# A decoder trunk on one core: decays' subtractions behind C B^T on VectorE, next weights behind the last operands, attention's output in natural column order

## The chip, the cores and the metric

The kernel runs on one core of a Trainium2 chip. Its engines are TensorE (PE, matrix products; PEld is its weight load), VectorE (DVE), ScalarE (ACT), GpSimd (POOL) and SyncE (SP, which issues the DMAs here). The metric is the device time of one execution in microseconds; the time of a kernel is the median of its runs. The profile is of one execution of its own.

## The reference

The input is one sequence of 512 tokens of width 1024, in float32. Two residual layers follow one another, each with a mixer and a gated convolutional feed-forward (FFN), each part behind an RMS norm; a last RMS norm ends it.

```python
for i in range(DEPTH):                       # DEPTH = 2
    h = rmsnorm(x, mix_norm_w[i])
    if i % 2 == 0: x = x + dilated_attention_mixer(...)   # 8 heads, 3 groups, dilations 1, 4, 16
    else:          x = x + ssd_mixer(...)                 # Mamba-2: 32 heads in 8 groups, chunks of 128
    h = rmsnorm(x, ffn_norm_w[i])
    x = x + conv_ffn(h, ...)                 # (silu(gate) * up) @ w_down, behind a causal convolution of 3
return rmsnorm(x, final_norm_w)
```

What matters of the Mamba-2 mixer: for each group the projections x, z, B and C; a causal convolution of four taps and SiLU on x, B and C; and then, for every chunk and head,

```python
seg    = a_cs[:, :, :, None] - a_cs[:, :, None, :]     # differences of running sums
lmat   = exp(where(causal, seg, -inf))
cb     = einsum("bcign,bcjgn->bcijg", cm, bm)          # C B^T of the group
y_diag = einsum("bcijgr,bcjgrp->bcigrp", cb[..., None] * lmat, xdt)
```

with the carried states added, the result gated by silu(z), normed per group and multiplied by w_out.

## The kernel before

**Products in three parts.** Every weight matrix comes as a unit of 128 x 1024 float32. `load_unit` (line 116) issues its DMA on SP into a buffer `raw` (4 of them), makes the high part `hi` by a cast on ACT (line 125) and the low part `lo = raw - hi` on DVE, or on the engine that `low` names (line 126; 5 buffers each). An operand is split likewise into `xh` (ACT, line 203) and `xl` (DVE, line 204). A product is then three matmuls (`mm3`, line 136): hi x xh, hi x xl, lo x xh. A tile of 128 x 512 over the width of 1024 is 8 x 3 = 24 matmuls, accumulated in one of three banks of PSUM called `mm`; there are three more called `aux` and two called `side`.

**Order.** The order on PE is written out by hand (`manual_schedule`). On the other engines a scheduler orders the instructions: of those that are ready by its own timing, the one first in the program. Each engine then works through its queue in that order. `tc.issue_after(ins)` puts what is traced inside it, as far as it is on the engine of `ins`, behind `ins` in that engine's queue; it sets an order and no wait, and binds no other engine, SP included. `queued(name)` (line 715) does this for the last instruction kept under a name.

**Attention.** Tokens are held in another order than the natural one: a column of the 512 stands for (n, r, l) = (block, residue, place). `attend(h)` (line 392) makes one head's scores, softmax and values; at its end line 491 copies the bank `pg` of the dilated groups to `o`, line 492 adds the bank `po`, and lines 494 and 495 split `o`. After the heads, the output projection `wo` adds to the residual `xr`, whose columns are natural: line 579 does it with a stride of 4 elements on `xr`, and `prep` splits `xr[m]` for the FFN.

**Entries.** `norm_and_project` (line 157) is the entry to a part behind a norm: it loads the first three units, multiplies the first seven eighths of two of them while the last split is still to come, then the rest, the norm's sum (line 226) and its inverse root along the columns. It is used before the first FFN (units u0 to u2) and before the Mamba mixer (xs00, wdt, b0). What follows is fetched by `project` (line 145) as it comes.

**The Mamba mixer.** `groups` (line 950) goes through eight groups. `behind(g)` steps the generator `scan_group(g)` (line 747) three times, and between the steps PE gets the tiles of `between(g)` (line 931): projections of the next group, and output products (`wso`) of past ones. Group 7 has no next one: between its first two steps stand four tiles of `wso` with 6 matmuls each, then z. Within `scan_group`:

- `decays` (line 782) runs a group ahead. It fetches rows of the running sums from DRAM, spread over the partitions, into four tiles `lm` (one for each head) and two `ee`. Sixteen ACT instructions (line 796: four tiles, four chunks) make relu(a_i - row), queued behind the last square of the group before (line 836); then, queued behind the last gate, come the exponentials of `ee` (line 799) and of `lm` (line 801).
- The first step: x transposed (`px`) and weighted by DVE (line 758) and POOL (line 759); B transposed (`pb`) and copied to `btok` by ACT (line 847); C B^T on PE (line 852), masked by DVE (line 854) to `cb`.
- The second: chunk states on PE from `btok` (line 769, bank `pst`), and lm x cb on POOL (line 862).
- The third: `products` on PE (lines 811, 819) and `outputs` on DVE and ACT (lines 829 to 836), and then the norm of the group.

The gates z0 and z1 are projected by `ssm_tile` (line 718), which makes their low parts on POOL. The results of `wso` leave PSUM by DVE (line 900).

Of the kernel before, what the change touches and what calls it, by code (L numbers as in the profile page):

```python
# [9 lines left out]
F32 = mybir.dt.float32  # L10
F32R = mybir.dt.float32r
AF = mybir.ActivationFunctionType
ALU = mybir.AluOpType

P = 128
# [7 lines left out]
DIL = 4  # L23
# [28 lines left out]
def trunk(ctx: ExitStack, tc: tile.TileContext, A, out):  # L52
    nc = tc.nc
    V, SC, G, T = nc.vector, nc.scalar, nc.gpsimd, nc.tensor
# [43 lines left out]
    xh = [cp.tile([P, S], F32R, tag=f"xh{k}", name=f"xh{k}") for k in range(KD)]  # L98
    cp.tile([P, 32], F32, tag="gap1", name="gap1")
    xl = [cp.tile([P, S], F32R, tag=f"xl{k}", name=f"xl{k}") for k in range(KD)]  # L100
# [9 lines left out]
    def col(c):  # L110
        return par[:, c : c + 1]
# [4 lines left out]
    def load_unit(src, name, n=1024, pieces=1, low=V, at=0):  # L116
        raw = wr.tile([P, 1024], F32, tag="raw", name=f"raw_{name}")
        hi, lo = (wh.tile([P, 1088], F32R, tag=t, name=f"{t}_{name}")[:, at : at + 1024] for t in ("hi", "lo"))
        for i in range(pieces):
            s = slice(i * n // pieces, (i + 1) * n // pieces)  # L120
            dma(raw[:, s], src[:, s])
            if i < pieces - 1:
                V.tensor_copy(hi[:, s], raw[:, s])
            else:
                SC.copy(hi[:, s], raw[:, s])  # L125
            low.tensor_tensor(lo[:, s], raw[:, s], hi.bitcast(F32)[:, s], op=ALU.subtract)  # L126
        return hi, lo
# [5 lines left out]
    def long_product(dst, w, x, first, last):  # L133
        T.matmul(in_turns(dst), w, in_turns(x), start=first, stop=last)  # L134

    def mm3(dst, hi, lo, at, rh, rl, first, last):
        w_h = hi[:, at * P : (at + 1) * P]
        w_l = lo[:, at * P : (at + 1) * P]
        long_product(dst, w_h, rh, first, False)
        long_product(dst, w_h, rl, False, False)  # L140
        long_product(dst, w_l, rh, False, last)

    early = {}

    def project(src, name, low=V, cut=None):

        if name in early:
            return early.pop(name)
        hi, lo = load_unit(src, name, low=low)
        t = mm_bank(name)  # L150
        for k in range(KD):
            if cut and cut[0] == k:
                cut[1]()
            mm3(t, hi, lo, k, xh[k], xl[k], k == 0, k == KD - 1)
        return t

    def norm_and_project(ssum, srcs):

        units = [(load_steps() if name == "wdt" else load_unit(src, name), mm_bank(name), name) for src, name in srcs]

        def part(i, ks):
            (hi, lo), t, name = units[i]
            for k in ks:
                if name == "wdt":
                    steps_products(t, hi, k)
                else:
                    mm3(t, hi, lo, k, xh[k], xl[k], k == 0, k == KD - 1)

        with tc.manual_schedule(engines={mybir.EngineType.PE}):
            part(0, range(KD - 1))  # L170
            part(1, range(KD - 1))
            part(0, [KD - 1])
            part(1, [KD - 1])
            inv_rms(ssum, D, rcol)
            part(2, range(5))
            p = along_free(rcol, "rb")
            SC.copy(rbc, p)
            part(2, range(5, KD))
        for _, t, name in units:
            early[name] = t  # L180
# [17 lines left out]
    def prep(k, src, c_w, ssum):  # L198
        split(k, src, c_w)
        square(k, src, ssum)  # L200

    def split(k, src, c_w):
        SC.activation(xh[k], src, AF.Copy, scale=col(c_w + k))
        V.scalar_tensor_tensor(  # L204
            xl[k], src, col(c_w + k), xh[k].bitcast(F32), op0=ALU.mult, op1=ALU.subtract
        )

    def square(k, src, ssum, add=G):
        if k == 0:
# [94 lines left out]
    ssum = t2("ssum", "ssum", 2)  # L304
# [45 lines left out]
    def in_blocks(ap):  # L350

        return ap.rearrange("p (n r l) -> p r n l", n=4, r=DIL)

    def by_residue(ap):
        return ap.rearrange("p (r n l) -> p r n l", n=4, r=DIL)

# [32 lines left out]
    scale = HD ** -0.5  # L389
    oh, ol = [], []  # L390

    def attend(h):
# [89 lines left out]
        po, pg = aux_bank(f"po{h}"), aux_bank(f"pg{h}")  # L482
# [5 lines left out]
        values(2)  # L488
        values(3)
        o = t2(f"o{h}", "o", 1, s3)  # L490
        SC.copy(in_blocks(o), by_residue(pg))
        V.tensor_tensor(o, o, po, op=ALU.add)
        o_h, o_l = high_low(f"o{h}")
        SC.copy(o_h, o)
        V.tensor_tensor(o_l, o, o_h.bitcast(F32), op=ALU.subtract)
# [70 lines left out]
    xr = [lp.tile([P, S], F32, tag=f"xr{k}", name=f"xr{k}") for k in range(KD)]  # L566
    for k in range(KD):
        dma(xr[k], A["xt"][k])

    def natural(ap):  # L570
        return ap.rearrange("p (n l r) -> p n r l", n=4, r=DIL)

    ssum = t2("ssum1", "ssum", 2)
    for m in range(KD):
        if m not in wo_held:
            wo_first(m)
        hi, lo, p = wo_held[m]
        mm3(p, hi, lo, NH - 1, oh[-1], ol[-1], False, True)
        V.tensor_tensor(
            natural(xr[m]), natural(xr[m]), p.rearrange("p (n r l) -> p n r l", n=4, r=DIL),  # L580
            op=ALU.add
        )
        prep(m, xr[m], C_FFN, ssum)


# [45 lines left out]
            with tc.manual_schedule(engines={mybir.EngineType.PE}):  # L631
                down(f"wd{layer}{part}", load, range(KD), lambda c: (gh[c], gl[c]), cn, add, late=True)

    def up_first(layer):
        return [(A["wup"][layer * 44 + i], f"u{layer}_{i}") for i in range(3)]

    norm_and_project(ssum, up_first(0))
    ssum_a = t2("ssum2", "ssum", 2)
    ffn(0, lambda m: prep(m, xr[m], C_MIX + KD, ssum_a))
    norm_and_project(ssum_a, [(A["win"][0], "xs00"), (A["wdt"], "wdt"), (A["win"][2], "b0")])  # L640


    def b3(ap, n):
# [8 lines left out]
    dtt, adt, acs, dec, cdec = (cst(n) for n in ("dtt", "adt", "acs", "dec", "cdec"))  # L652
# [60 lines left out]
    latest = {}  # L713

    def queued(name):
        return tc.issue_after(latest.pop(name).ins) if name in latest else nullcontext()

    def ssm_tile(i, c_conv, name):
        p = project(A["win"][i], name, V if c_conv is not None else G)
        us = t2("us" + name, *(("a", 13) if c_conv is None else ("us", 3)), lp)  # L720
        with queued("mean"):
            V.tensor_tensor(us, p, rbc, op=ALU.mult)
        if c_conv is None:
            with queued("decay"):
                latest["gate"] = SC.activation(us, us, AF.Silu)
            return us
        a = t2("a" + name, "a", 13, lp)
        conv(a, us, C_SCW + c_conv * 4, C_SCB + c_conv, 4)
        with queued("decay"):
            SC.activation(a, a, AF.Silu)  # L730
        return a
# [15 lines left out]
    def scan_group(g, d, ys):  # L747
# [3 lines left out]
        xdt, xdd, prev, ee, lm = [], [], [], [], []  # L751
# [30 lines left out]
        def decays():  # L782

            for x in range(2):
                ee.append(t2("ee", "ee", 2, lp))
                for hp in range(2):
                    h, half = heads[x].start + hp, slice(hp * 64, (hp + 1) * 64)
                    t = t2("lm", "lm", 4, lp)
                    dma(t, rows[h : h + 1, :].to_broadcast([P, S]))
                    dma(ee[x][half, P:512], rows[h : h + 1, P:512].to_broadcast([64, S - P]))  # L790
                    lm.append(t)
            with queued("square"):
                for i, t in enumerate(lm):
                    for c in range(NCH):
                        cs, at = slice(c * P, (c + 1) * P), c * NSH + heads[0].start + i
                        SC.activation(t[:, cs], t[:, cs], AF.Relu, bias=acs[:, at : at + 1], scale=-1.0)
            with queued("gate"):
                for x in range(2):
                    SC.activation(ee[x][:, P:512], ee[x][:, P:512], AF.Exp)
                for t in lm:  # L800
                    latest["decay"] = SC.activation(t, t, AF.Exp, scale=-1.0)

        def products(x):

# [22 lines left out]
        def outputs(x, py, pf):  # L827
            yt = t2("yt", "yt", 2, lp)
            V.tensor_tensor(ee[x][:, P:512], ee[x][:, P:512], pf[:, P:512], op=ALU.mult)
            V.scalar_tensor_tensor(  # L830
                yt, xs[x], col(C_DSK + 2 * g + x), py, op0=ALU.mult, op1=ALU.add
            )
            V.tensor_tensor(yt[:, P:512], yt[:, P:512], ee[x][:, P:512], op=ALU.add)
            V.tensor_tensor(yt, yt, d[f"z{x}"], op=ALU.mult)
            sq = t2("gsq", "sq", 2)
            latest["square"] = SC.activation(sq, yt, AF.Square)
            return yt, sq

        decays()
# [10 lines left out]
        for c in range(NCH):  # L850
            cs = slice(c * P, (c + 1) * P)
            T.matmul(pc[:, cs], bt[:, cs], ct[:, cs], start=True, stop=True)
        cb = t2("cb", "cb", 1, lp)
        V.tensor_tensor(
            cb.rearrange("p (c i) -> p c i", c=NCH), pc.rearrange("p (c i) -> p c i", c=NCH),
            tri.unsqueeze(1).to_broadcast([P, NCH, P]), op=ALU.mult,
        )
        yield
        for x in range(2):
            states(x)  # L860
# [336 lines left out]
```

## Time and profile before

| | us |
|---|---|
| median of 3 runs (1650.4 to 1650.81) | 1650.46 |
| the profiled execution | 1650.0 |
| its span, first to last instruction | 1648.2 |
| PE busy in it | 1634.3 |
| DVE, ACT, POOL busy | 1042.8, 695.7, 459.2 |

A row of the profile names a line, an engine, an operation, `out<-in` by the program's names, a shape and a count. PE's matmuls are pipelined: a row may show 0.38 us, while the next one starts 0.22 later. A bracket such as `[2.36 <-ACT btok L847]` says that the engine sat idle for 2.36 us and what ended it. PEclk is the clock granted to TensorE, 1.00 being full speed. 99% busy for PE is not PE at its peak: products at a lower clock count as busy too.

### The profile page before, as it was taken

How to read it: one execution, taken by the hardware profiler on the slowest of the kernel's cores; microseconds unless marked ns; L12 is line 12 of the kernel's file. 1: busy time of each engine (PE TensorE's matmuls, PEld its weight loads, DVE VectorE, ACT ScalarE, POOL GpSimd, SP SyncE). 2: the span in 40 equal slices, each digit the busy share in tenths (PEclk: the TensorE clock that was granted, in tenths of full speed). 3: DMA queues.
4: the chain of work that ended last, by engine and by line, in shares of the span. 5: the costliest groups of instructions: out<-in, count | busy, mean ns of one | idle time of the engine just before them, and what ended most of it. 6: DMA issues, size and time to landing. Idle time of an engine off the chain costs nothing.

```text
span 1648.2 us, 21517 instructions
## 1 busy us (share of the span) xinstructions
PE 1634.3 (99%) x8236; PEld 1402.5 (85%) x8236; DVE 1042.8 (63%) x1672; ACT 695.7 (42%) x1115; POOL 459.2 (28%) x294
## 2 busy tenths in 40 slices
PE   9999999999999999999999999999999999999998
PEld 8888888888888888888888888888878888888888
DVE  6366665366658745755656677776776684574565
ACT  5233332333245423433445745555562552343345
POOL 0444443144503211220232322332230341121022
PEclk9999999999999999999999999999999999999999
DMA  7322222222223323223234333233432332332323
GB/s 255 103 77 77 82 86 90 90 80 87 77 90 128 103 89 115 96 87 112 77 106 132 107 112 101 83 106 112 138 112 66 101 104 89 115 103 90 106 74 128
DMA packets 54390, 168.32 MB, mean 102 GB/s; under 512 B 6352, under 2 KB 9808, under 8 KB 54288
## 3 DMA queue, kind: packets, MB, share of 16 engines
q1 hardware_dynamic: 53456, 166.15, 30.0%
q8 instruction: 65, 1.06, 0.3%
q10 hardware_dynamic: 832, 0.79, 0.1%
q14 instruction: 37, 0.30, 0.1%
HBM read 164.76 MB, written 2.16 MB: 101 GB/s over the span
## 4 chain that ended last, share of the span: by engine, by line
PE 94%; DVE 2%; ACT 2%; issue 1%; DMA 0%; POOL 0%; DVEq 0%; POOLq 0%; ACTq 0%
PE u L134 28%; PE qk L134 15%; PE wd L134 12%; PE v L134 8%; PE xs L134 5%; PE z L134 5%; PE wso L134 4%; PE b L134 2%; PE c L134 2%; PE wo L134 2%; PE wz L134 1%; PE py L811 1%; PE pg L468 1%; PE pp L455 1%; PE po L463 1%
## 5 line engine op out<-in xcount | busy, mean ns | idle before, releaser
L134 PE MATMUL u<-xh,lo_u 128*128 128x512 f32 x704 | 269.0, 382 | 0.0
L134 PE MATMUL u<-xh,hi_u 128*128 128x512 f32 x704 | 268.7, 382 | 0.0
L134 PE MATMUL u<-xl,hi_u 128*128 128x512 f32 x704 | 266.4, 378 | 0.3 <-DVE xl L204 0.3
L611 POOL TENSOR_TENSOR au<-au,au 128x512 f32<-128x512 f32 x43 | 56.8, 1322 | 423.9 <-DVE au L589 397.4
L589 DVE SCALAR_TENSOR_TENSOR au<-usu,par,au 128x510 f32<-128x510 f32 (+1 forms) x176 | 160.9, 919 | 6.2 <-ACT au L587 1.3
L125 ACT CAST hi_u<-raw_u 128x1024 fp32r<-128x1024 f32 x88 | 91.2, 1044 | 170.7 <-PE u L134 97.1
L366 POOL TENSOR_TENSOR rotqk<-rotqk,sr 32x512 f32<-32x512 f32 x48 | 90.0, 1874 | 251.8 <-DVE rotqk L365 241.4
L134 PEld LDWEIGHTS u<-xl,hi_u 128*128 128x128 f32 x704 | 131.7, 187 | 25.2 <-DVE xl L204 0.7
L134 PEld LDWEIGHTS u<-xh,lo_u 128*128 128x128 f32 x704 | 131.7, 187 | 24.0
L134 PEld LDWEIGHTS u<-xh,hi_u 128*128 128x128 f32 x704 | 131.7, 187 | 21.3
L134 PE MATMUL qk<-xh,hi_qk 128*128 128x512 f32 x384 | 148.6, 387 | 0.0
L134 PE MATMUL qk<-xh,lo_qk 128*128 128x512 f32 x384 | 147.1, 383 | 0.0
L134 PE MATMUL qk<-xl,hi_qk 128*128 128x512 f32 x384 | 145.6, 379 | 0.0
L126 DVE TENSOR_TENSOR lo_u<-raw_u,hi_u 128x1024 fp32r<-128x1024 f32 x88 | 110.1, 1256 | 25.9 <-ACT hi_u L125 25.9
L604 DVE TENSOR_TENSOR usu<-u,rbc 128x512 f32<-128x512 f32 x88 | 60.5, 690 | 103.0 <-PE u L134 93.7
L125 ACT CAST hi_qk<-raw_qk 128x1024 fp32r<-128x1024 f32 x48 | 50.3, 1047 | 135.4 <-PE qk L134 73.9
L624 DVE TENSOR_TENSOR xr<-xr,wd 128x512 f32<-128x512 f32 x40 | 27.2, 688 | 117.1 <-PE wd L134 117.1
L125 ACT CAST hi_wd<-raw_wd 128x1024 fp32r<-128x1024 f32 (+1 forms) x56 | 52.5, 952 | 90.3 <-PE wd L134 55.9
L134 PEld LDWEIGHTS qk<-xh,lo_qk 128*128 128x128 f32 x384 | 71.8, 187 | 13.3
L134 PEld LDWEIGHTS qk<-xl,hi_qk 128*128 128x128 f32 x384 | 71.9, 187 | 12.7
L362 DVE TENSOR_TENSOR qk<-qk,cr 128x512 f32<-128x512 f32 x48 | 33.0, 688 | 77.9 <-PE qk L134 77.7
L134 PEld LDWEIGHTS qk<-xh,hi_qk 128*128 128x128 f32 x384 | 71.9, 187 | 11.3
(641 smaller groups left out, 3925.4 us busy)
## 6 DMA issues: line engine op xcount, KB each, us to landing
raw_u<-in_wup SPq DMA_DIRECT2D x88, 512.0 KB, 3.2
raw_qk<-in_wqk SPq DMA_DIRECT2D x48, 512.0 KB, 3.2
raw_wd<-in_wdn SPq DMA_DIRECT2D x32, 512.0 KB, 3.2
raw_wd<-in_wdn SPq DMA_DIRECT2D x24, 384.0 KB, 3.0
raw_xs<-in_win SPq DMA_DIRECT2D x16, 512.0 KB, 3.2
raw_z<-in_win SPq DMA_DIRECT2D x16, 512.0 KB, 4.0
lm<-rows SPq DMA_DIRECT2D x32, 256.0 KB, 5.5
raw_wso<-in_wso SPq DMA_DIRECT2D x16, 512.0 KB, 3.2
```

The costliest lines, as they stand in the source:

```text
L125: SC.copy(hi[:, s], raw[:, s])
L126: low.tensor_tensor(lo[:, s], raw[:, s], hi.bitcast(F32)[:, s], op=ALU.subtract)
L134: T.matmul(in_turns(dst), w, in_turns(x), start=first, stop=last)
L362: V.tensor_tensor(at(t), of(p), of(cr), op=ALU.mult)
L366: G.tensor_tensor(rot[R, :], rot[R, :], sr[R, :], op=ALU.mult)
L455: T.transpose(pp[:, b * P : (b + 1) * P], pr[:, b * P : (b + 1) * P], ident)
L463: T.matmul(po[:, ii], v0[h][:, b * P : (b + 1) * P], pts[i][:, (b - i + 1) * P : (b - i + 2) * P], start=b == max(i - 1, 0), stop=b == i,)
L468: T.matmul(pg[:, ii], vt[g, half][i][:, es], pts[i][:, (g + 1) * P : (g + 2) * P], start=g == 1, stop=g == 2,)
L589: V.scalar_tensor_tensor(dst[:, j:], src[:, : S - j], col(c_w + taps - 1 - j), dst[:, j:], op0=ALU.mult, op1=ALU.add,)
L604: V.tensor_tensor(us, p, rbc, op=ALU.mult)
L611: by.tensor_tensor(ab[1], ab[0], ab[1], op=ALU.mult)
L624: V.tensor_tensor(xr[m], xr[m], p, op=ALU.add)
```

## The change

Four edits. First, `norm_and_project` gets a list `more`: the next two units are loaded at the entry, with their casts on ACT and their low parts on DVE queued behind the last split's two instructions. Second, attention writes `o` in natural column order, so lines 491 and 492 get the stride and line 579 loses it. Third, the gates' low parts go to DVE, as with all other units. Fourth, the differences of the decays are made by DVE, as min(row - a_i, 0), queued behind the masking of the same group's C B^T; the exponentials follow, `lm` first (behind the last gate) and `ee` behind them, and nothing is queued behind the square any more.

```diff
@@ -140,13 +140,14 @@
         long_product(dst, w_h, rl, False, False)
         long_product(dst, w_l, rh, False, last)
 
+    loaded = {}
     early = {}
 
     def project(src, name, low=V, cut=None):
 
         if name in early:
             return early.pop(name)
-        hi, lo = load_unit(src, name, low=low)
+        hi, lo = loaded.pop(name) if name in loaded else load_unit(src, name, low=low)
         t = mm_bank(name)
         for k in range(KD):
             if cut and cut[0] == k:
@@ -154,7 +155,7 @@
             mm3(t, hi, lo, k, xh[k], xl[k], k == 0, k == KD - 1)
         return t
 
-    def norm_and_project(ssum, srcs):
+    def norm_and_project(ssum, srcs, more):
 
         units = [(load_steps() if name == "wdt" else load_unit(src, name), mm_bank(name), name) for src, name in srcs]
 
@@ -165,6 +166,10 @@
                     steps_products(t, hi, k)
                 else:
                     mm3(t, hi, lo, k, xh[k], xl[k], k == 0, k == KD - 1)
+
+        with tc.issue_after(last_split[0].ins), tc.issue_after(last_split[1].ins):
+            for src, name in more:
+                loaded[name] = load_unit(src, name)
 
         with tc.manual_schedule(engines={mybir.EngineType.PE}):
             part(0, range(KD - 1))
@@ -199,11 +204,15 @@
         split(k, src, c_w)
         square(k, src, ssum)
 
+    last_split = []
+
     def split(k, src, c_w):
-        SC.activation(xh[k], src, AF.Copy, scale=col(c_w + k))
-        V.scalar_tensor_tensor(
-            xl[k], src, col(c_w + k), xh[k].bitcast(F32), op0=ALU.mult, op1=ALU.subtract
-        )
+        last_split[:] = [
+            SC.activation(xh[k], src, AF.Copy, scale=col(c_w + k)),
+            V.scalar_tensor_tensor(
+                xl[k], src, col(c_w + k), xh[k].bitcast(F32), op0=ALU.mult, op1=ALU.subtract
+            ),
+        ]
 
     def square(k, src, ssum, add=G):
         if k == 0:
@@ -351,6 +360,10 @@
 
         return ap.rearrange("p (n r l) -> p r n l", n=4, r=DIL)
 
+    def natural(ap):
+
+        return ap.rearrange("p (n l r) -> p n r l", n=4, r=DIL)
+
     def by_residue(ap):
         return ap.rearrange("p (r n l) -> p r n l", n=4, r=DIL)
 
@@ -488,8 +501,8 @@
         values(2)
         values(3)
         o = t2(f"o{h}", "o", 1, s3)
-        SC.copy(in_blocks(o), by_residue(pg))
-        V.tensor_tensor(o, o, po, op=ALU.add)
+        SC.copy(o.rearrange("p (n l r) -> p r n l", n=4, r=DIL), by_residue(pg))
+        V.tensor_tensor(natural(o), natural(o), po.rearrange("p (n r l) -> p n r l", n=4, r=DIL), op=ALU.add)
         o_h, o_l = high_low(f"o{h}")
         SC.copy(o_h, o)
         V.tensor_tensor(o_l, o, o_h.bitcast(F32), op=ALU.subtract)
@@ -567,19 +580,13 @@
     for k in range(KD):
         dma(xr[k], A["xt"][k])
 
-    def natural(ap):
-        return ap.rearrange("p (n l r) -> p n r l", n=4, r=DIL)
-
     ssum = t2("ssum1", "ssum", 2)
     for m in range(KD):
         if m not in wo_held:
             wo_first(m)
         hi, lo, p = wo_held[m]
         mm3(p, hi, lo, NH - 1, oh[-1], ol[-1], False, True)
-        V.tensor_tensor(
-            natural(xr[m]), natural(xr[m]), p.rearrange("p (n r l) -> p n r l", n=4, r=DIL),
-            op=ALU.add
-        )
+        V.tensor_tensor(xr[m], xr[m], p, op=ALU.add)
         prep(m, xr[m], C_FFN, ssum)
 
 
@@ -631,13 +638,13 @@
             with tc.manual_schedule(engines={mybir.EngineType.PE}):
                 down(f"wd{layer}{part}", load, range(KD), lambda c: (gh[c], gl[c]), cn, add, late=True)
 
-    def up_first(layer):
-        return [(A["wup"][layer * 44 + i], f"u{layer}_{i}") for i in range(3)]
-
-    norm_and_project(ssum, up_first(0))
+    def ups(layer, some):
+        return [(A["wup"][layer * 44 + i], f"u{layer}_{i}") for i in some]
+
+    norm_and_project(ssum, ups(0, range(3)), ups(0, (3, 4)))
     ssum_a = t2("ssum2", "ssum", 2)
     ffn(0, lambda m: prep(m, xr[m], C_MIX + KD, ssum_a))
-    norm_and_project(ssum_a, [(A["win"][0], "xs00"), (A["wdt"], "wdt"), (A["win"][2], "b0")])
+    norm_and_project(ssum_a, [(A["win"][0], "xs00"), (A["wdt"], "wdt"), (A["win"][2], "b0")], [(A["win"][3], "c0"), (A["win"][1], "xs01")])
 
 
     def b3(ap, n):
@@ -716,7 +723,7 @@
         return tc.issue_after(latest.pop(name).ins) if name in latest else nullcontext()
 
     def ssm_tile(i, c_conv, name):
-        p = project(A["win"][i], name, V if c_conv is not None else G)
+        p = project(A["win"][i], name)
         us = t2("us" + name, *(("a", 13) if c_conv is None else ("us", 3)), lp)
         with queued("mean"):
             V.tensor_tensor(us, p, rbc, op=ALU.mult)
@@ -789,16 +796,19 @@
                     dma(t, rows[h : h + 1, :].to_broadcast([P, S]))
                     dma(ee[x][half, P:512], rows[h : h + 1, P:512].to_broadcast([64, S - P]))
                     lm.append(t)
-            with queued("square"):
+
+        def exponentials(masked):
+
+            with tc.issue_after(masked.ins):
                 for i, t in enumerate(lm):
                     for c in range(NCH):
                         cs, at = slice(c * P, (c + 1) * P), c * NSH + heads[0].start + i
-                        SC.activation(t[:, cs], t[:, cs], AF.Relu, bias=acs[:, at : at + 1], scale=-1.0)
+                        V.tensor_scalar(t[:, cs], t[:, cs], acs[:, at : at + 1], 0.0, op0=ALU.subtract, op1=ALU.min)
             with queued("gate"):
-                for x in range(2):
-                    SC.activation(ee[x][:, P:512], ee[x][:, P:512], AF.Exp)
-                for t in lm:
-                    latest["decay"] = SC.activation(t, t, AF.Exp, scale=-1.0)
+                last = [SC.activation(t, t, AF.Exp) for t in lm][-1]
+            with tc.issue_after(last.ins):
+                for t in ee:
+                    latest["decay"] = SC.activation(t[:, P:512], t[:, P:512], AF.Exp)
 
         def products(x):
 
@@ -833,7 +843,7 @@
             V.tensor_tensor(yt[:, P:512], yt[:, P:512], ee[x][:, P:512], op=ALU.add)
             V.tensor_tensor(yt, yt, d[f"z{x}"], op=ALU.mult)
             sq = t2("gsq", "sq", 2)
-            latest["square"] = SC.activation(sq, yt, AF.Square)
+            SC.activation(sq, yt, AF.Square)
             return yt, sq
 
         decays()
@@ -851,10 +861,11 @@
             cs = slice(c * P, (c + 1) * P)
             T.matmul(pc[:, cs], bt[:, cs], ct[:, cs], start=True, stop=True)
         cb = t2("cb", "cb", 1, lp)
-        V.tensor_tensor(
+        masked = V.tensor_tensor(
             cb.rearrange("p (c i) -> p c i", c=NCH), pc.rearrange("p (c i) -> p c i", c=NCH),
             tri.unsqueeze(1).to_broadcast([P, NCH, P]), op=ALU.mult,
         )
+        exponentials(masked)
         yield
         for x in range(2):
             states(x)
```

## The prediction

> **What bounds the kernel now.** I read the page first, then the waits of TensorE (PE), then PE's order of time at each wait, and last the windows around them. The page says that PE is the bound, with little left to win:
>
> ```profile
> span 1648.2 us, 21517 instructions
> PE 1634.3 (99%) x8236; PEld 1402.5 (85%) x8236; DVE 1042.8 (63%) x1672; ACT 695.7 (42%) x1115; POOL 459.2 (28%) x294
> ```
>
> So a change off PE can only take away PE's waits. There are few (us in total, times, longest):
>
> ```profile
> PE wso L134 <- DVE xr L900: 3.3, 1, 3.3
> PE pst L769 <- ACT btok L847: 2.4, 1, 2.4
> ...
> PE xs L134 <- DVE xl L204: 0.6, 1, 0.6
> PE u L134 <- DVE xl L204: 0.3, 1, 0.3
> ```
>
> PE's order of time at each (start, us, what), then windows (busy us of PE, PEld, DVE, ACT, POOL, then the granted clock):
>
> ```profile
> 507.59 0.38 PE L134 MATMUL u<-xh,hi_u 128*128 128x512 f32 x1
> 508.30 0.49 PE L134 MATMUL u<-xl,hi_u 128*128 128x512 f32 x1 [0.33 <-DVE xl L204]
> ...
> 858.73 0.38 PE L134 MATMUL xs<-xh,hi_xs 128*128 128x512 f32 x1
> 859.68 0.49 PE L134 MATMUL xs<-xl,hi_xs 128*128 128x512 f32 x1 [0.57 <-DVE xl L204]
> ...
> 992.70 0.38 PE L134 MATMUL c<-xl,hi_c 128*128 128x512 f32 x1
> 992.92 0.38 PE L134 MATMUL c<-xh,lo_c 128*128 128x512 f32 x1
> 995.66 2.19 PE L769 MATMUL pst<-xdd,btok 128*128 128x128 f32 x12 [2.36 <-ACT btok L847]
> ...
> 1227.98 0.38 PE L134 MATMUL wso<-y41h,lo_wso 128*128 128x512 f32 x1
> 1231.65 0.53 PE L134 MATMUL wso<-y40h,hi_wso 128*128 128x512 f32 x1 [3.29 <-DVE xr L900]
> ```
> ```profile
> 855.00:900.00 45.00, 44.43 (x216) 36.38 (x215) 28.95 (x50) 22.39 (x31) 11.40 (x6) 1.00 0.32 106
> ...
> 995.70:1003.30 7.60, 7.60 (x30) 6.73 (x31) 7.01 (x6) 4.42 (x6) 5.98 (x4) 0.55 0.22 71
> ...
> 1231.60:1235.40 3.80, 3.75 (x10) 2.97 (x11) 3.38 (x5) 1.86 (x3) 3.80 (x4) 0.55 0.78 237
> ...
> 1040.00:1091.00 51.00, 51.00 (x285) 43.96 (x284) 36.63 (x53) 27.81 (x51) 14.12 (x9) 1.00 0.33 112
> ```
>
> An unhindered product follows its forerunner by 0.22 us (992.70 to 992.92). From start to start, less 0.22, the waits cost 0.49 (508), 0.73 (859), 2.52 (995) and 3.45 us (1231). Behind the two long ones the clock stands at 0.55 for 7.60 and 3.80 us, another 0.45 x 7.60 = 3.42 and 0.45 x 3.80 = 1.71. Behind the 0.73 it stays at 1.00. The four are worth 0.49, 0.73, 5.94 and 5.16: 12.3 us in all is the most that the change can win.
>
> The Trainium skill, "TensorE: Matmul & The Clock Gate", Part 1, has the clock halved after an idle window of about 3.4 us and released after such a window of work. Here 2.52 us was enough, so the measurement decides; by the page alone the wait at 995 would be worth 2.5, and the forecast below 3.4 us higher.
>
> **The change part by part.** *Next weights behind the last operands.* Two casts on ACT and two low parts on DVE go behind the last split, at both entries. At either entry DVE has such low parts in front of a late xl (at the second lo_c stands before the two rows shown, as long as lo_xs):
>
> ```profile
> 506.36 1.22 DVE L126 TENSOR_TENSOR lo_u<-raw_u,hi_u 128x1024 fp32r<-128x1024 f32 x1
> ...
> 856.70 1.22 DVE L126 TENSOR_TENSOR lo_xs<-raw_xs,hi_xs 128x1024 fp32r<-128x1024 f32 x1
> 857.84 3.46 DVE L204 SCALAR_TENSOR_TENSOR xl<-xr,par,xh 128x512 fp32r<-128x512 f32 x2
> ```
>
> Without them xl starts near 855.5 (857.84 - 2 x 1.15) and PE wants it at 858.95: the 0.73 goes, and so does the 0.49 at 508, where one lo_u of 1.22 is more than the wait (and the adds are faster, below). What comes late is lo_c, by some 3 us, and its products start only behind the three tiles of the entry. The DMAs of the two loads sit on SP, which the order doesn't bind; each holds its raw buffer about 3 us longer, and SP's next loads slip by that. Cost 0; 0.7 us at either entry if the cover is gone.
>
> *Order of columns in attention.* The stride moves from line 579 to line 492 (its out and one input in natural order, the other from PSUM), and the write of line 491 gets one too:
>
> ```profile
> L579 DVE TENSOR_TENSOR xr<-xr,wo x8: 1169/1188/1208, 484.8 to 508.2; 128x512 f32<-128x512 f32 x8
> ...
> L624 DVE TENSOR_TENSOR xr<-xr,wd x40: 686/689/690, 602.8 to 1541.0; 128x512 f32<-128x512 f32 x40
> ...
> L491 ACT COPY o<-pg x8: 585/585/587, 133.7 to 474.8; 128x512 f32<-128x512 f32 x8
> ...
> 140.94 0.69 DVE L362 TENSOR_TENSOR qk<-qk,cr 128x512 f32<-128x512 f32 x1 [3.99 <-PE qk L134]
> ```
>
> Line 579 falls from 1.19 to 0.69, line 492 rises by the same 0.50, eight times each. The strided ACT write isn't in the trace: between 0.585 and, by DVE's ratio of 1.72, 1.01 us; I take 1.0. Both lie in front of idle time of DVE such as the 3.99 us in the last row, behind the first head, so 0; without that cover 8 x 0.92 = 7.4.
>
> *Gates' low parts.* Sixteen leave POOL (2.38 each, below) for 1.22 each on DVE: 2.4 us more for each group, where DVE is busy for 36.63 of 51.
>
> *Decays.* Per group ACT loses 16 pieces of Relu, and DVE gets 16 subtractions of 128x128 directly behind cb; the exponentials follow these, no longer the square. At 995 this is decisive:
>
> ```profile
> 987.27 4.78 ACT L796 ACTIVATE lm<-lm,acs 128x128 f32<-128x128 f32 x16
> ...
> 995.06 0.46 ACT L847 COPY btok<-pb 128x384 f32<-128x384 f32 x1
> ```
>
> ACT has no idle time in front of btok (no bracket in its row): it stood in the queue and waited for no input. Without the block of 4.78 it starts at 990.3 at the latest, and sooner as the exponentials between them move behind cb; PE wants it at 993.1. The 5.94 go. In return DVE's queue holds 16 subtractions before the next evictions of PSUM. Their price, from the nearest kind (eight, seven of them 128x256 with a scalar per partition):
>
> ```profile
> 115.72 2.13 DVE L452 TENSOR_SCALAR pr<-pr,join 128x128 f32<-128x128 f32 x8
> ```
>
> At most 0.27 each, at least half of that; I take 0.2, so 3.2 us (2.1 to 4.3). In groups 0 to 6 the next eviction belongs to a tile whose 24 products take 24 x 0.22 = 5.3 us, and three banks stand ready: cost 0. In group 0 the subtractions also wait for rows from DRAM:
>
> ```profile
> 901.18 0.58 SPq L789 DMA_DIRECT2D lm<-rows  x1
> ...
> lm<-rows SPq DMA_DIRECT2D x32, 256.0 KB, 5.5
> ```
>
> They land near 906.7, so DVE may stand there for a few us; the same 5.3 us and the banks cover it. Only group 7 is tight: it starts with tiles of 6 products (1.32 us).
>
> ```profile
> 1220.14 2.38 POOL L126 TENSOR_TENSOR lo_z<-raw_z,hi_z 128x1024 fp32r<-128x1024 f32 x1 [20.08 <-ACT hi_z L125]
> ...
> 1220.63 2.45 DVE L868 TENSOR_TENSOR gsq<-gsq 128x512 f32<-128x512 f32 x1 [0.96 <-ACT gsq L836]
> ...
> 987.39 0.69 DVE L868 TENSOR_TENSOR gsq<-gsq 128x512 f32<-128x512 f32 x1 [2.78 <-ACT gsq L836]
> ...
> 1225.39 0.67 DVE L854 TENSOR_TENSOR cb<-pc,tri 128x512 f32<-128x512 f32 x1
> ...
> 1229.54 1.46 DVE L126 TENSOR_TENSOR lo_wso<-raw_wso,hi_wso 128x1024 fp32r<-128x1024 f32 x1 [3.40 <-ACT hi_wso L125]
> 1230.93 0.67 DVE L900 TENSOR_TENSOR xr<-xr,wso 128x512 f32<-128x512 f32 x1
> ```
>
> Before, the eviction stood behind lo_wso, and that behind a cast that came late on ACT (3.40 idle), where the Relus are. Now: gsq drops from 2.45 to 0.69 with lo_z off POOL, lo_z adds 1.22, so cb ends 0.5 earlier than at 1226.06, at 1225.5; 16 subtractions to 1228.7; the eviction to 1229.4. PE wants the bank at 1228.2: 1.2 us stay (0 if the order puts the eviction first). That lies nearer to 0.73, which left the clock alone, than to 2.52, so I count no slow clock. Saved: 5.16 - 1.2 = 3.96.
>
> Sum: 0.49 + 0.73 + 5.94 + 3.96 = 11.1 from the profiled execution's 1650.0 (its span and 1.8 around it) is 1638.9; the median of the runs, 1650.46, stands 0.46 above, so 1639.3.
>
> **The rivals.** *POOL and the subtractions hold each other up.* Convolution steps of DVE show it:
>
> ```profile
> 945.85 5.46 POOL L862 TENSOR_TENSOR lm<-lm,cb 128x512 f32<-128x512 f32 x4
> ...
> 948.35 6.28 DVE L589 SCALAR_TENSOR_TENSOR axs<-usxs,par,axs 128x511 f32<-128x511 f32 x3 [5.42 <-ACT axs L587]
> ...
> 970.39 2.31 DVE L589 SCALAR_TENSOR_TENSOR axs<-usxs,par,axs 128x511 f32<-128x511 f32 x3
> ```
>
> Three steps took 6.28 beside POOL's products and 2.31 alone. If the subtractions take turns with three of those (5.46 / 4 = 1.37 each), the block is 3.2 + 4.1 = 7.3, the eviction ends at 1233.5, and PE waits 5.3 with 1.71 to 3.42 of slow clock: 7.0 to 8.7 for 5.16. Time 1639.3 + 3.96 + 1.8 to 3.6 = 1645.1 to 1646.8. Against it: line 452 has no POOL work beside it in the trace, so nothing shows the turn for one-input operations. The Trainium skill, "SBUF — State Buffer", "Who interferes with whom", calls the pair of ports that VectorE and GpSimd share an exclusive lock, also for one-input operations in a two-port mode; by that rule this rival holds. The rows above agree with it for steps with two inputs; for one input no run here shows it yet. Chance 0.20.
>
> *Group 7 keeps its wait*, as lo_wso or other work stays before the eviction: 1639.3 + 3.96 = 1643.3, 0.15. *btok stays late*, since the table load and exponentials come before it: 1639.3 + 5.94 = 1645.2; against it, they are now bound behind cb; 0.08. *Both stay*, the chain only changing its member: 1649.2, no change; 0.08.
>
> *Slower: DVE becomes the bound of the groups.* Of 51 us DVE has 36.63; subtractions 3.2, low parts 2.4, turns with POOL 4.1 there and 4.0 (6.28 - 2.31) at the steps make 50.3. From about 51 on every further us is paid in each of seven groups; from 1.5 us a group on (10.5 over 1643.3) the kernel is slower than before by over 0.2%; at 2 us it takes 1657. Against it: the 4.0 is already in the 36.63 in part. Chance 0.08.
>
> **How the numbers follow.** The forecast has 0.41: 1639.3, by itself 1637.5 (no wait left in group 7, and slivers) to 1641.0 (the slow clock's 1.71 added). The range of 1637.0 to 1647.2 takes in all but "both stay" and "slower" (0.84). A change of under 0.2% (3.3 us) is about what a measurement can't tell from none: faster 0.84, same 0.08, slower 0.08.
>
> **What would show it.** Right: PE's waits on btok and on xl gone, the clock at 1.00 from 990 to 1005, line 796's ACT rows gone, and 16 rows of about 0.2 on DVE behind each cb. Group 7's step is right if PE's wait on xr is under 1.5 us. Wrong: subtractions of over 0.4 us beside POOL, a wait of PE on xr of over 3 us with a clock under 1.00 behind it, PE waiting for DVE's evictions in groups 1 to 6, or line 492 in a chain of waits in attention.

## The result: 1640.4 us, 0.6% faster than before

| | before | after |
|---|---|---|
| median of four runs | 1650.45 us (1650.40 to 1650.81) | 1640.37 us (1639.92 to 1641.27) |
| ratio of the times | | 0.9942, 95% interval 0.9929 to 0.9954 |
| span of the profiled execution | 1648.2 us | 1638.4 us |
| mean granted clock of TensorE | 0.996 | 0.999 |

The forecast was 1639.3, from 1637.0 to 1647.2. The sum came out within 1.1 us; the experiments show that two of its terms had been put down to the wrong part of the change. The page of the changed kernel, its first two lines:

```profile
span 1638.4 us, 21542 instructions
PE 1628.0 (99%) x8236; PEld 1398.8 (85%) x8236; DVE 1084.4 (66%) x1816; ACT 663.5 (40%) x985; POOL 420.7 (26%) x278
```

PE still is the bound, and DVE has 42 us more. What PE waits for now (us in total, times, longest), all rows:

```profile
PE wso L134 <- DVE xr L911: 2.5, 1, 2.5
PE warm L318 <- DVE mhalf L107: 1.1, 1, 1.1
PE ss L235 <- DVE ssum L223: 0.3, 1, 0.3
PE ss L235 <- ACT sq L1059: 0.2, 1, 0.2
```

btok and both rows with xl are gone. PE's order of time at the four places (the second operand at either entry, then pst, then group 7), and the windows behind them (busy us of PE, PEld, DVE, ACT, POOL, then the granted clock):

```profile
507.40 0.38 PE L134 MATMUL u<-xl,hi_u 128*128 128x512 f32 x1
...
857.87 0.38 PE L134 MATMUL xs<-xl,hi_xs 128*128 128x512 f32 x1
...
991.24 0.49 PE L776 MATMUL pst<-xdd,btok 128*128 128x128 f32 x3
...
1219.66 0.38 PE L134 MATMUL wso<-y41h,lo_wso 128*128 128x512 f32 x1
1222.55 0.49 PE L134 MATMUL wso<-y40h,hi_wso 128*128 128x512 f32 x1 [2.51 <-DVE xr L911]
```
```profile
990.00:1005.00 15.00, 15.00 (x91) 12.93 (x91) 13.80 (x25) 8.97 (x14) 4.22 (x2) 1.00 0.22 72
...
1222.60:1230.00 7.40, 7.40 (x36) 6.30 (x37) 3.44 (x5) 2.39 (x4) 4.83 (x4) 1.00 0.22 71
1074.00:1125.00 51.00, 51.00 (x285) 43.96 (x284) 40.67 (x72) 23.29 (x33) 7.85 (x7) 1.00 0.34 111
```

Three of the four places have no bracket: PE doesn't wait there, and the clock stands at 1.00. One wait stays, in group 7: from start to start 2.89 us, less 0.22, so 2.67 instead of the 1.2 forecast. DVE has 40.67 busy us in a group of 51 (36.63 before; the rival that ends slower had added up 50.3), short of being the bound.

PE runs the same 8236 products in the same order in both kernels, so the start of each can be set against its own start before. The changed kernel is ahead by 1.2 us at 516, 1.9 at 860, 8.0 at 1010, 10.6 at 1240, and 10.2 at the last sum of squares: the gain lies at the four waits of the forecast, 1.2 + 0.7 + 6.0 + 2.7, with 0.4 given back at the end.

DVE's queue in group 7 of the changed kernel, and POOL's beside it:

```profile
1216.72 0.68 DVE L864 TENSOR_TENSOR cb<-pc,tri 128x512 f32<-128x512 f32 x1
1217.32 4.51 DVE L806 TENSOR_SCALAR lm<-lm,acs 128x128 f32<-128x128 f32 x16
1221.75 0.15 DVE L240 TENSOR_SCALAR ms<-ss 128x4 f32<-128x4 f32 x1
1221.82 1.87 DVE L911 TENSOR_TENSOR xr<-xr,wso 128x512 f32<-128x512 f32 x3
```
```profile
1215.15 2.57 POOL L766 TENSOR_TENSOR xdd<-xdt,dec 128x384 f32<-128x384 f32 x2 [30.64 <-DVE xdt L765]
1220.46 3.76 POOL L873 TENSOR_TENSOR lm<-lm,cb 128x512 f32<-128x512 f32 x3 [2.74 <-ACT lm L808]
```

The eviction stands directly behind the block. The 16 subtractions take 4.51 us, not 3.2. Singly, 14 of them take 0.28 each and start every 0.20; the first, beside xdd, takes 0.48, and the last, which starts at 1220.46 with POOL's product, 1.37. Over all groups:

```profile
L806 DVE TENSOR_SCALAR lm<-lm,acs x128: 273/279/1399, 903.5 to 1220.5; 128x128 f32<-128x128 f32 x128
```

Of the 128, 15 last longer than 0.4 us, and each of them ends 0.08 to 0.09 behind the end of an instruction of POOL. In the first three groups it is three of sixteen, as rival one had it; in group 2, DVE and then POOL:

```profile
985.88 4.20 DVE L806 TENSOR_SCALAR lm<-lm,acs 128x128 f32<-128x128 f32 x4
```
```profile
985.82 3.98 POOL L873 TENSOR_TENSOR lm<-lm,cb 128x512 f32<-128x512 f32 x3 [2.77 <-ACT lm L808]
```

Three turns of 1.1 cost PE nothing there. In group 7 POOL's first product began only with the last subtraction, so there was one. By the signs that the prediction named, btok, xl and the clock came out right; the long subtractions are one of its signs of being wrong, and group 7's wait of 2.51 is over the 1.5 that it had set for that step.

### The profile page after: what moved, and what is told of

The parts are those of the page before. It is cut to its first block, busy times and chain, and to the rows that moved or that the text cites. A ratio compares the mean times of both kernels' runs of the same rounds, so it can differ in the third digit from the quotient of the medians.

```text
span 1638.4 us, 21542 instructions
## 1 busy us (share of the span) xinstructions
PE 1628.0 (99%) x8236; PEld 1398.8 (85%) x8236; DVE 1084.4 (66%) x1816; ACT 663.5 (40%) x985; POOL 420.7 (26%) x278
## 4 chain that ended last, share of the span: by engine, by line
PE 98%; DVE 1%; issue 0%; ACT 0%; DMA 0%; POOL 0%; DVEq 0%; POOLq 0%; ACTq 0%
PE u L134 28%; PE qk L134 16%; PE wd L134 12%; PE v L134 8%; PE xs L134 5%; PE z L134 5%; PE wso L134 5%; PE b L134 3%; PE wo L134 3%; PE c L134 3%; PE wz L134 1%; PE py L821 1%; PE pg L481 1%; PE pp L468 1%; PE po L476 1%; PE pf L829 1%
## 5 line engine op out<-in xcount | busy, mean ns | idle before, releaser
L766 POOL TENSOR_TENSOR xdd<-xdt,dec 128x384 f32<-128x384 f32 x16 | 18.0, 1140 | 254.1 <-DVE xdt L765 254.1
L126 DVE TENSOR_TENSOR lo_qk<-raw_qk,hi_qk 128x1024 fp32r<-128x1024 f32 x48 | 60.9, 1269 | 32.4 <-ACT hi_qk L125 32.4
```

The source lines that it names most:

```text
L766: G.tensor_tensor(v4(u[:, 0:384], 3), v4(t[:, 0:384], 3), b3(dec3[:, 0:3, heads[x]], 64), op=ALU.mult)
```

## Experiments

Theory after the result: each part does what the forecast says, and group 7's rest is the block in DVE's queue with one turn of POOL (a turn is the time by which an instruction lasts longer because it stands beside one of another engine). Rivals: that another part than the one named takes a wait away, and that the long subtractions have another cause than POOL. First each part was undone alone in the changed kernel.

**The old entry.**
```
-        with tc.issue_after(last_split[0].ins), tc.issue_after(last_split[1].ins):
-            for src, name in more:
-                loaded[name] = load_unit(src, name)
```


> The changed kernel without its first part: the two next units of weights are loaded where their tile is, no longer behind the last split. Theory (the low parts stood in front of a late xl): PE's waits for xl come back at both entries, up to 0.49 us at about 508 and 0.73 us at about 859, so about 1.2 us longer than the changed kernel's 1640.4, near 1641.6. Since the adds of the attention's end are 0.5 us faster each now, the first of the two may be smaller. Rival (the waits went with the other parts, and this part is idle): no PE wait for xl in the trace and no more time, 1640.4.

1642.32 us (1641.24 to 1642.68). Of PE's waits that for xl at the second entry is back, the first is not:

```profile
PE wso L134 <- DVE xr L907: 2.5, 1, 2.5
...
PE xs L134 <- DVE xl L208: 0.6, 1, 0.6
```

So this part is worth the 0.73 of the second entry. The rest of the 1.95 is not this part's: in this run the same wait of group 7 was followed by a slow clock (0.63 from 1222.7 to 1227.3), see the last section.

**The old order of columns.**
```
-        SC.copy(o.rearrange("p (n l r) -> p r n l", n=4, r=DIL), by_residue(pg))
-        V.tensor_tensor(natural(o), natural(o), po.rearrange(...), op=ALU.add)
+        SC.copy(in_blocks(o), by_residue(pg))
+        V.tensor_tensor(o, o, po, op=ALU.add)
...
-        V.tensor_tensor(xr[m], xr[m], p, op=ALU.add)
+        V.tensor_tensor(natural(xr[m]), natural(xr[m]), p.rearrange(...), op=ALU.add)
```


> The changed kernel with the old order of columns at the attention's end and at the adds behind it. Theory (both sides hidden): ACT's copy of the attention's output falls from 1.12 to 0.59 us, the add behind it from 1.15 to 0.69, the eight later adds rise from 0.68 to 1.19, and the time stays within 0.5 us of 1640.4. Rival (the later adds are what made the entry's last operand early): PE's wait for xl at about 508 comes back with 0.3 to 0.5 us, 1640.9. Other rival (the slower copies in attention cost PE): the time falls by up to 8 x 1 us, to 1632.

1641.84 us (1641.21 to 1642.44): 1.5 more (1641.21 in the profiled execution). Set against the changed kernel, PE is 0.1 behind up to 430, 0.95 at 508 (0.28 of it in one piece, in front of the first entry's xl) and about 1.0 from there on. So the first entry's wait went with the faster adds, not with the next weights. In attention nothing is won back by the faster copy, although ACT's strided copy is dearer than taken (changed kernel):

```profile
L504 ACT COPY o<-pg 128x512 f32<-128x512 f32 x8 | 9.0, 1124 | 8.4 <-PE pg L481 8.4
```

**The gates' low parts on POOL again.**
```
-        p = project(A["win"][i], name)
+        p = project(A["win"][i], name, V if c_conv is not None else G)
```


> The changed kernel with the gates' 16 low parts back on POOL. Theory (worth only what it brings before the subtractions of group 7): the add of the two squares takes 2.4 us again instead of 0.69 and one low part of 1.2 us leaves DVE in front of it, so the 16 subtractions start about 0.5 us later and PE's wait for xr grows from 2.5 to about 3.0 us; nothing else: 1640.9. If the low parts on POOL fall beside subtractions, those pay turns of 2.4 us, which show as single subtractions of that length, and the wait could grow to 5, with slow clock behind it: 1643 to 1646. Rival (DVE's load in the groups counts): DVE is relieved by 16 x 1.22 us and PE waits less: under 1640.

1646.48 us (1645.68 to 1647.25): 6.1 more, far over the 0.5 expected. Set against the changed kernel, PE loses 0.3 of it at 1021 and the rest in group 7:

```profile
PE wso L134 <- DVE xr L911: 6.2, 1, 6.2
...
PE ss L235 <- DVE gsq L879: 1.0, 1, 1.0
```

with 6.83 us of half clock behind it. Why it is so much more than 0.5 shows in DVE's rows, then POOL's:

```profile
1191.22 2.10 DVE L596 SCALAR_TENSOR_TENSOR ab<-usb,par,ab 128x511 f32<-128x511 f32 x1
...
1213.33 2.43 DVE L879 TENSOR_TENSOR gsq<-gsq 128x512 f32<-128x512 f32 x1 [0.96 <-ACT gsq L846]
...
1220.94 5.60 DVE L806 TENSOR_SCALAR lm<-lm,acs 128x128 f32<-128x128 f32 x16
```
```profile
1190.38 2.39 POOL L126 TENSOR_TENSOR lo_z<-raw_z,hi_z 128x1024 fp32r<-128x1024 f32 x1 [6.38 <-ACT hi_z L125]
1212.85 2.36 POOL L126 TENSOR_TENSOR lo_z<-raw_z,hi_z 128x1024 fp32r<-128x1024 f32 x1 [20.07 <-ACT hi_z L125]
```

The two DVE steps beside low parts take 2.10 and 2.43 (0.75 and 0.69 in the changed kernel), cb ends at 1221.0 instead of 1217.4, and the block holds two turns instead of one. The expectation counted the second of the two steps and not the first.

**The old decays.**
```
-                        V.tensor_scalar(t[:, cs], t[:, cs], acs[:, at : at + 1], 0.0, op0=ALU.subtract, op1=ALU.min)
+                        SC.activation(t[:, cs], t[:, cs], AF.Relu, bias=acs[:, at : at + 1], scale=-1.0)
```
(with the old queues: behind the square, exponentials of ee first)

> The changed kernel with the old decays: the pieces with Relu on ACT, queued behind the square, and the exponentials as before; the three other parts stay. Theory (this part carries nearly all): the block of 4.8 us of ACT stands before btok in group 2 again, PE waits 2.4 us for it there, and about 3.3 us in group 7, with the clock at 0.5 for one or two stretches of 3.41 us behind each: 5.9 + 5.2 - 2.7 = 8.4 us more, 1648.8. Rival (the gates' low parts on DVE make the add of the squares, and so the block, early enough): btok's wait stays away and only group 7 costs, 1640 to 1643.

1640.43 us (1639.30 to 1641.32), within 0.1 of the changed kernel. The part that the forecast gave nearly ten microseconds is worth nothing as long as the gates' low parts are on DVE. The waits are others, and as long:

```profile
PE pst L776 <- ACT btok L854: 1.1, 1, 1.1
PE warm L318 <- DVE mhalf L107: 1.1, 1, 1.1
PE wso L134 <- DVE usz L729: 0.8, 1, 0.8
...
PE wso L134 <- DVE xr L907: 0.2, 1, 0.2
```

btok's wait is half of before (start to start less 0.22: 1.29 for 2.52), too short for a slow clock; group 7's is nearly gone.

**Either part alone, in the kernel before** (the edits above, the other way round).

> The kernel before with one part of the change alone: the gates' 16 low parts on DVE. Theory, from the kernel without the new decays (the low parts on POOL are what made the square and the blocks behind it late): btok's wait falls from 2.4 to 1.1 us without slow clock behind it (another 1 us shows at about 1023), group 7's from 3.3 to under 1 without slow clock; the two waits for xl stay: -5.9 + 1.6 + 1.0 - 5.2 + 0.4 = -8.1, so 1642.4. Rival (the account of the recorded prediction, where this part was worth 0.5 us in group 7): 1649.5 to 1650.

1642.51 us (1641.96 to 1643.32), against 1650.23 of the kernel before, measured beside it: 7.7 won by 16 instructions that change their engine.

> The kernel before with the new decays alone (subtractions on DVE behind cb, exponentials behind them). Theory, from the kernel with the gates' low parts back on POOL: btok's wait is gone (-5.9), group 7's wait is 6.2 us with 6.8 us of slow clock behind it and 1 us for the square (+4.5 to 5.5 over the 5.2 of before); the waits for xl stay: 1649 to 1650.5. Rival (the recorded prediction's account: 5.9 + 3.5 to 4 won): 1640.5 to 1641.

1648.83 us (1648.15 to 1650.04): 1.4 less by the medians and not clear of noise, ratio 0.9992 (0.9983 to 1.0001). btok's wait is gone, and group 7 takes the gain back: 6.2 us there for 3.3 before. Both parts take away the wait at 995, so they can't be added; in group 7 the gates' part helps and the decays' part harms.

Why 16 instructions matter is read from the kernel before, DVE first, then POOL:

```profile
980.49 2.32 DVE L833 TENSOR_TENSOR yt<-yt,ee 128x384 f32<-128x384 f32 x2
...
1198.51 2.11 DVE L589 SCALAR_TENSOR_TENSOR ab<-usb,par,ab 128x511 f32<-128x511 f32 x1
```
```profile
979.55 2.37 POOL L126 TENSOR_TENSOR lo_z<-raw_z,hi_z 128x1024 fp32r<-128x1024 f32 x1 [13.37 <-ACT hi_z L125]
...
1197.67 2.39 POOL L126 TENSOR_TENSOR lo_z<-raw_z,hi_z 128x1024 fp32r<-128x1024 f32 x1 [3.78 <-ACT hi_z L125]
```

and from the one with the gates' part alone:

```profile
980.25 1.02 DVE L833 TENSOR_TENSOR yt<-yt,ee 128x384 f32<-128x384 f32 x2
...
1193.90 0.74 DVE L589 SCALAR_TENSOR_TENSOR ab<-usb,par,ab 128x511 f32<-128x511 f32 x1
```

Each of these steps of DVE, with both inputs in SBUF, meets a low part on POOL and lasts until that is through: 1.30 and 1.37 us longer. The first lies in the chain yt, square, block of ACT, btok: btok's wait is shorter by 1.59 in the kernel with the gates' part alone (0.77 for 2.36). If that is the cause, moving these two of the 16 (z30 and z70, the first gates of groups 3 and 7) takes one turn off each wait:

```
-        p = project(A["win"][i], name, V if c_conv is not None else G)
+        p = project(A["win"][i], name, V if c_conv is not None or name in ("z30", "z70") else G)
```


> The kernel before, with two of the gates' 16 low parts on DVE and 14 left on POOL: the one that ran at 979.6 beside the add of ee to yt (2.32 us for two instead of 1.02) and the one at 1197.7 beside a convolution step (2.11 us instead of 0.74). Theory (what the part is worth lies in the turns that POOL's low parts take from steps of DVE that lie in front of ACT's blocks, and these two are they): btok's wait falls by the 1.3 us of the first turn, to 1.2, and loses its slow clock (4.6 in all, perhaps 1 of it given back at about 1029), and group 7's wait falls by at least the 1.35 us of the second, to at most 2.1 and with little or no slow clock (1.4 to 4.5): 1642.3 to 1645.4. Rival (the gain is that of the load of all 16, shared out): two of 16 bring a little over 1 us, 1649 to 1650.4.

1646.26 us (1644.60 to 1647.21), 3.6 under the kernel before (1649.9, measured beside it). The longest waits of its profiled execution, which took 1645.20:

```profile
PE wso L134 <- DVE xr L900: 2.0, 1, 2.0
PE wso L134 <- DVE usz L722: 1.2, 2, 0.8
PE pst L769 <- ACT btok L847: 1.1, 1, 1.1
...
PE b L134 <- DVE usxs L722: 0.5, 1, 0.5
```

Both waits fall by one turn, btok's from 2.4 to 1.1 and group 7's from 3.3 to 2.0, as expected; neither has a slow clock behind it in this execution. The median misses its range by 0.9. The eleven runs fall into five from 1644.6 to 1645.7 (mean clock 0.999) and six from 1646.3 to 1647.2 (0.998). A stretch of slow clock behind group 7's wait in the six would fit (see the last section), but none of them was profiled. In the profiled execution 2.2 us come back at 1026, 1078 and 1084, where PE now waits for DVE's usz and usxs; 1.0 of it was expected, and why the rest comes wasn't followed up. Two of the 16 thus bring about half of the 7.7. In group 7 a third turn is left, beside a low part that stayed on POOL:

```profile
1216.47 2.50 DVE L868 TENSOR_TENSOR gsq<-gsq 128x512 f32<-128x512 f32 x1 [0.96 <-ACT gsq L836]
```

It takes 0.69 with all 16 on DVE, where group 7's wait is 0.2 instead of 2.0. That this turn, and others like it, make up the rest is likely, and no run shows it alone.

**The block of group 7.** Does POOL's product make the last subtraction long?

```
-        for t in lm:
+        for t in lm[::-1] if g == NSG - 1 else lm:
```


> The changed kernel, but in group 7 POOL multiplies the four decay tiles in reverse order, so its first product needs the last of the exponentials and can't begin before the subtractions are through. Theory (a subtraction that meets a product on POOL waits its 1.3 us turn): all 16 subtractions of group 7 take 0.28 us, the block 3.4 instead of 4.5, and PE's wait for xr falls by 1.1 us from 2.5 to 1.4: 1639.3. Rival (the long last subtraction has another cause, such as its input): it stays at 1.37 us and the wait at 2.5, 1640.4.

1639.71 us (1639.14 to 1640.53), wait 2.5 and last subtraction 1.36, as before. It says nothing: the scheduler put the products back into their old order. With the order tied (each product issued behind the one before it):

> The experiment with the reversed products again, the order now tied by hand: in group 7 alone POOL's four products run from the last decay tile to the first, so the first needs the last exponential and meets no subtraction. Theory (a subtraction that meets a product on POOL waits its 1.3 us turn): all 16 subtractions take 0.28 us (the first one 0.48, beside the end of xdd), the block 3.4 us instead of 4.5, PE's wait for xr 1.4 us instead of 2.5: 1639.3, and no run with slow clock behind it. Rival (the long last subtraction has another cause, such as its input): it stays at 1.37 us and the wait at 2.5: 1640.4.

1638.66 us (1638.37 to 1638.95). The block and the wait:

```profile
1217.08 3.43 DVE L806 TENSOR_SCALAR lm<-lm,acs 128x128 f32<-128x128 f32 x16
1220.42 0.15 DVE L240 TENSOR_SCALAR ms<-ss 128x4 f32<-128x4 f32 x1
1220.50 1.87 DVE L913 TENSOR_TENSOR xr<-xr,wso 128x512 f32<-128x512 f32 x3
```
```profile
PE wso L134 <- DVE xr L913: 1.4, 1, 1.4
```

1.1 less in both. The turn with POOL is shown.

**The eviction first.** In group 7 alone the subtractions go behind the evictions of two output tiles:

```
-        exponentials(masked)
+        if g == NSG - 1:
+            held_back.append(lambda: exponentials(latest.pop("wso")))
+        else:
+            exponentials(masked)
...
-                V.tensor_tensor(xr[m], xr[m], p, op=ALU.add)
+                latest["wso"] = V.tensor_tensor(xr[m], xr[m], p, op=ALU.add)
...
+                    if held_back and j == 1:
+                        held_back.pop()()
```


> The changed kernel, but in group 7 alone the 16 subtractions are queued on DVE behind the evictions of the first two tiles of the output projection, no longer directly behind cb. Theory (the 4.5 us block of subtractions in DVE's queue is all that keeps the bank from PE): the first eviction goes at about 1217.5 (PE ends that tile at 1217.4), the second at 1218.9, the subtractions from 1219.5 to 1222.7 or 1223.8; PE's wait of 2.51 us is gone, and with it the slow stretch behind it in those runs that had one; py wants the products at 1242, so their being 2 us later costs nothing: 2.7 to 3.5 us less than 1640.4, 1637 to 1637.8. Rival (something else is as late): a wait for another tile, low part or btok of 1 us or more takes its place, 1639 to 1640.4.

1636.75 us (1636.63 to 1636.88): 0.992 of the kernel before (0.9906 to 0.9933) and 3.6 us under the changed kernel, the best version of this study. 2.7 of the 3.6 are the wait, and the rest is small differences at the start and the end. DVE in group 7, and PE where it waited:

```profile
1217.20 0.69 DVE L915 TENSOR_TENSOR xr<-xr,wso 128x512 f32<-128x512 f32 x1
1218.52 0.69 DVE L915 TENSOR_TENSOR xr<-xr,wso 128x512 f32<-128x512 f32 x1 [0.63 <-PE wso L134]
1219.13 4.34 DVE L807 TENSOR_SCALAR lm<-lm,acs 128x128 f32<-128x128 f32 x16
```
```profile
1219.42 0.38 PE L134 MATMUL wso<-y41h,lo_wso 128*128 128x512 f32 x1
1219.64 0.38 PE L134 MATMUL wso<-y40h,hi_wso 128*128 128x512 f32 x1
```

The products follow each other by 0.22. The block is as long as before, still with one turn, and costs nothing.

## Why the prediction was right, and where it was not

*Next weights and the entries: half right.* Both waits went. But the 0.49 at 508 went with the faster adds (the order of columns, which was counted at 0 and is worth about 1.0), and only the 0.73 at 859 with this part. The forecast had the remark that the adds get faster in its text, and not in its sum.

*Order of columns: the cover held, two sizes were off.* The strided copy on ACT takes 1.12, over the upper bound of 1.01: DVE's ratio of 1.72 did not carry over to ACT, which has 1.92. No wait in attention came of it.

*Gates' low parts: the step that failed.* They were costed as load, 2.4 us more per group on DVE, and as 1.76 of gsq less a low part of 1.22 in group 7. Their worth is 6.1 us (undone) to 7.7 (alone). The row was in the forecast: three convolution steps of 6.28 beside POOL and 2.31 alone. It was used for a rival, against the change; of the 16 instructions that leave POOL the forecast asked it of one (gsq in group 7), and not of the others. The Trainium skill, "SBUF — State Buffer", "Who interferes with whom", has a step of VectorE with two inputs in SBUF contend with a GpSimd instruction that reads SBUF, for ports that are an exclusive lock. The trace agrees (2.32 for 1.02 at 980), and the one-input subtractions pay too (1.37 for 0.28), which the forecast left open. The trace of the kernel before had such a case: seven times in attention a small TENSOR_SCALAR with one input lasts 0.56 us instead of 0.16 and ends 0.03 behind POOL's line 367:

```profile
104.78 0.56 DVE L422 TENSOR_SCALAR neg<-own 128x2 f32<-128x2 f32 x1
```

*Decays: the mechanism right, the credit wrong.* btok did stand behind the block of 4.78, and without it the wait is gone (shown by the decays alone). But the 5.94 were not the decays' own: an earlier block is enough, and the gates' part brings that. As one of two causes it got the whole price. Undone, it costs 0.1; alone, it brings 1.4, not clear of noise.

*Group 7: the term mis-sized, 2.5 saved for 3.96.* The block took 4.51 for 3.2: one subtraction paid a turn of 1.1, which was rival one's mechanism at a quarter of its 4.1 (in groups 0 to 2 three subtractions paid, as that rival had it, but nothing waited there), and the first 0.2 beside xdd. With the turn taken away, 2.67 - 1.08 = 1.59 is left, against the 1.2 forecast. The clause in the forecast, 0 if the order puts the eviction first, is what the last experiment shows. No slow clock came in the profiled execution, as forecast, but by luck: the wait of 2.67 is longer than the 2.52 that had one, so by the forecast's own reason (nearer to 0.73 than to 2.52) it should have come; see below.

The total held because it was a sum of waits measured in the trace, not of the worth of parts: whichever part takes a wait away, it can't bring more than it. That it came within 1.1 us is luck in part: 1.5 too much in group 7 and 0.4 given back at the end stand against 0.7 too little at 508, and 6.1 of the gain hang on the gates' part, which the forecast gave 0.5.

## To carry to other kernels

Before a step is moved off an engine, ask which instructions of the other engines it lengthens where it stands: such a turn shows as a longer duration of the other instruction and in no list of waits, so compare the slowest rows of a group with its median and see what runs beside them. Two edits that remove the same wait can't be added; undo each alone before either gets the credit. A block of small instructions in a queue belongs behind the evictions that PE needs next, not in front of them.

## What the runs showed of the hardware

*The clock is judged in fixed stretches that run free of the program.* In all profiles of this case the recorded changes of TensorE's clock lie whole multiples of 3.413 us apart (996.45, 1003.27, 1231.97, 1235.38 in the kernel before), while the first comes 4.05 to 7.06 us after the start, another time in each execution. A wait therefore costs by how it falls into these stretches. The changed kernel's wait was split into 1.82 and 0.68 and left the clock at 1.00; the same wait in the kernel with the old entry was split into 0.21 and 2.29 and halved it for 3.41 us. In the ten profiles in which PE waits 1 us or more behind the start, at most 1.86 us of idle time in one stretch never slowed the clock, and 2.29 and more did in all five cases; nothing between was met. The runs of one kernel show it too: those of the old entry lie at 1641.2 to 1641.5 (mean clock 0.999) and at 1642.3 to 1642.7 (0.998), while the kernel with the products last, whose wait of 1.4 is too short, has all five within 0.6. The mean clock alone is no proof: the kernel with the eviction first, which has no such wait, has runs at 0.999 and at 0.998 within 0.3 us. The Trainium skill, "TensorE: Matmul & The Clock Gate", Part 1, has the free-running window of 3413 ns, which agrees; that an idle window is needed does not: 2.29 of 3.41 us were enough. Why the slow stretch is one window behind some waits (3.10 idle) and two behind others (2.36) stays open.

*No turn was seen with one input in PSUM.* cb's product, with one input in PSUM, lay beside POOL's xdd in every group of the changed kernel and took 0.68 to 0.69 each time, while subtractions and steps with both inputs in SBUF paid turns of up to 1.8 (gsq 2.50 for 0.69).
